# Feature-major latent queries, five whole gate blocks between the latent units, and T sums in quarters, in a hybrid decoder layer

## The chip, the cores and the metric

The kernel runs on one core of a Trainium2 chip. A core has TensorE (PE in the profile, with its weight loads as PEld), VectorE (DVE), ScalarE (ACT), GpSimd (POOL) and SyncE (SP), which here only issues DMAs; ACT issues some too. All DMAs run on the core's 16 DMA engines. The metric is the time of one execution in device microseconds (us), as the median of a few runs; lower is better.

## The reference, cut to what matters

One layer on 1024 tokens of width 1024, all in float32. Two token mixers run in parallel on `h = rmsnorm(x)`: sparse attention (NSA), and latent attention (MLA). Their outputs are merged by sigmoid gates, and a gated ConvFFN follows.

```python
proj = h @ w_in                       # 1024 x 3768: q_n, kv_n, gate_n, c_q, c_kv, k_r, merge
gm = sigmoid(merge)                   # 2048 columns: 16 blocks of 128, the "gate blocks"
q = (rmsnorm(c_q, g_q) @ w_uq).reshape(B, T, 8, 64 + 32)      # latent queries, 256 -> 768
q_rope = rope(q[..., 64:], cos, sin)  # x1*cos - x2*sin, x2*cos + x1*sin, halves of 16
kv = (rmsnorm(c_kv, g_kv) @ w_ukv).reshape(B, T, 8, 64 + 64)  # k_nope and v, 128 -> 1024
s = (q_nope @ k_nope.T + q_rope @ rope(k_r).T) * 96 ** -0.5   # causal softmax, then @ v
merged = gm[0] * (o_nsa @ w_br_nsa) + gm[1] * (o_mla @ w_br_mla)
```

## The kernel before, in words

Precision. Every large product is made of three fp32r matmuls (`mm3`, lines 303 to 305): an operand is split into a rounded high part (ACT copies it, L308) and a low part, the difference (DVE, L309; both in `split_evac`). For weights of class `Weights` the two instructions are L106 and L107.

Order. The kernel is written as a sequence of loops, but a planner sorts the instructions of each engine by priority (the written order) and by when it thinks that their inputs are ready. The run order is thus near the written one without being equal to it. Each engine then works in order. Tiles come from pools; a pool opened after others were closed takes their space, and its tiles wait for the old tiles that lay there. Left-side and right-side pools grow towards one another.

Stages up to the change. (1) The loop over the eight 128-token tiles: `prep(t)` normalises a tile and transposes it to feature-major `hh`/`hl` (high and low, two halves of 512 tokens), `tok1(t)` computes gate_n, c_q, c_kv and k_r, and `tok1_tr(t)` transposes the latents to `cth`/`ctl` (three chunks of 128 features by 1024 tokens). `xn` is a two-buffer tile of that loop. Positions give `sin` and `cos` with tokens on partitions. (2) `fproj(merge_evac(0))`: gate block 0. A whole gate block is two halves of 512 tokens, each of 8 x 3 matmuls of 512 columns; ACT takes the sigmoid, and the block goes to `gm_d` in DRAM by a DMA from ACT. (3) The latent stage, from `a2 = Pool("a2")`. For each token tile `mla_q` makes 8 x 96 query features with tokens on partitions (two matmul groups of 384 columns), ACT scales them into `qm` (L609), six DVE instructions turn the rotary part (L615 to L620), `mla_qt` transposes the eight heads (L627) and stores both parts to `q_d` in runs of 512 bytes (L630). `mla_v` makes the values of a token tile and stores them to `v_d`, by heads, in runs of 512 bytes (L639); `mla_k` makes the keys of two heads and 512 tokens and stores them to `k_d` in runs of 2 KB (L648). The store tiles `qx`, `vm`, `kx` have 3, 2 and 2 buffers. (4) Gate blocks. `EARLY` = 1, 2 and 13 are computed whole; blocks 3 to 12 in five pairs by class `Seven`, a seven-product scheme (Strassen-Winograd) over quarters: a product is 12 matmuls, a pair 84. It needs sums of the right operand, `t_block`: T1 = B12 - B11, T2 = B22 - T1, T3 = B22 - B12, T4 = B21 - T2, where B are quarters of `hh`/`hl`, and each T has four chunks of 512 columns. A chunk takes three DVE instructions (L675 to L677) and a split (L308, L309). For the weights, `block_sum` (L170) makes the S sums and `prep` the splits, in a ring of four. In the first pair the products come in the order P1, P2, P3, P5, P6, P7, P4 and need B11, B21, B22, T1, T2, T3, T4.

PSUM banks for single results come from `bank()`, three buffers (`pT`), and pairs of banks from `two_banks()`, two buffers (`sc`).

Weights. `Weights.get` splits an item and `ahead` more, and issues loads (L81, on SP's queue) for up to three raw buffers beyond, in the order in which the items were added. Split parts have two buffers.

Stages behind the change. Projections for NSA, its attention, then MLA attention in 15 visits of heads (`mla_unit`). `mla_load` (L1059 to L1062) fetches a head's keys, queries and values on SP's queue, one visit ahead; a tile is free for the visit after next. The output branches follow, then the ConvFFN and the rest, which the change doesn't touch.

Of the kernel before, what the change touches and what calls it, by code (L numbers as in the profile page):

```python
# [17 lines left out]
T = 1024  # L18
# [257 lines left out]
def tile_hybrid_layer(ctx: ExitStack, tc: tile.TileContext, x, p, positions, g_pre_mix, w_in,  # L276
# [81 lines left out]
    EARLY, PAIRED = (1, 2, 13), range(3, 13)  # L358
# [57 lines left out]
    gmp = Pool("gmp", side="right")  # L416
    a0 = Pool("a0", side="right")
# [130 lines left out]

    def fproj2(evacs):
# [35 lines left out]

    a2 = Pool("a2", side="right")
    wuh, wul = a2([128, 2, 768], F32R, "wuh"), a2([128, 2, 768], F32R, "wul")
    wkh, wkl, wvh, wvl = (a2([128, 8, 64], F32R, n) for n in ("wkh", "wkl", "wvh", "wvl"))
    scale_m = float(96.0 ** -0.5)

# [5 lines left out]
    for k, it in enumerate(uq_items):  # L596
        it.alloc = into(wuh[:, k], wul[:, k])
# [3 lines left out]
    def mla_q(t):  # L601
        ts = slice(t * 128, (t + 1) * 128)
        qm = a2([128, 8, 96], F32, "qm", bufs=3)
        for hf in range(2):
            ps = bank()
            hs = slice(hf * 384, (hf + 1) * 384)
            for k in range(2):
                mm3(ps[:, :384], cth[:, k, ts], ctl[:, k, ts], wuh[:, k, hs], wul[:, k, hs], k == 0, k == 1)
            nc.scalar.activation(qm[:, 4 * hf:4 * hf + 4], ps[:, :384].rearrange("p (h d) -> p h d", d=96),  # L609
                                 AF.Copy, scale=scale_m)  # L610
        x1, x2 = qm[:, :, 64:80], qm[:, :, 80:96]
        cb = cos[:, t, None, :].to_broadcast([128, 8, 16])
        sb = sin[:, t, None, :].to_broadcast([128, 8, 16])
        ra, rb = (a2([128, 8, 32], F32, n, bufs=2) for n in ("ra", "rb"))
        nc.vector.tensor_tensor(ra[:, :, :16], x1, cb, op=OP.mult)  # L615
        nc.vector.tensor_tensor(ra[:, :, 16:], x2, cb, op=OP.mult)
        nc.vector.tensor_tensor(rb[:, :, :16], x2, sb, op=OP.mult)
        nc.vector.tensor_tensor(rb[:, :, 16:], x1, sb, op=OP.mult)
        nc.vector.tensor_sub(x1, ra[:, :, :16], rb[:, :, :16])
        nc.vector.tensor_add(x2, ra[:, :, 16:], rb[:, :, 16:])  # L620
        return qm

    def mla_qt(t, qm):
        ts = slice(t * 128, (t + 1) * 128)
        ps = two_banks().rearrange("p a (b m) -> p (a b) m", m=128)
        for h in range(8):
            nc.tensor.transpose(ps[:96, h], qm[:, h], ident)  # L627
        qx = a2([96, 8, 2, 128], F32R, "qx", bufs=3)
        split_evac(qx[:, :, 0], qx[:, :, 1], ps[:96])
        nc.sync.dma_start(q_d.rearrange("h n p t -> p (h n) t")[:, :, ts], f32(qx).rearrange("p h n t -> p (h n) t"))  # L630

    def mla_v(t):
        ts = slice(t * 128, (t + 1) * 128)
        ps = bank()
        vh, vl = (w.rearrange("p h d -> p (h d)") for w in (wvh, wvl))
        mm3(ps, cth[:, 2, ts], ctl[:, 2, ts], vh, vl, True, True)
        vm = a2([128, 8, 128], F32R, "vm", bufs=2)
        split_evac(vm[:, :, 0:64], vm[:, :, 64:128], ps.rearrange("p (h d) -> p h d", d=64))
        nc.sync.dma_start(v_d.rearrange("h t p d -> t p h d")[t], f32(vm))  # L639

    def mla_k(pr, c):
        cs = slice(c * 512, (c + 1) * 512)
        ps = bank()
        wh, wl = (w[:, 2 * pr:2 * pr + 2].rearrange("p h d -> p (h d)") for w in (wkh, wkl))
        mm3(ps, wh, wl, cth[:, 2, cs], ctl[:, 2, cs], True, True)
        kx = a2([128, 2, 512], F32R, "kx", bufs=2)
        split_evac(kx[:, 0], kx[:, 1], ps)
        nc.sync.dma_start(k_d[pr].rearrange("n p t -> p n t")[:, :, cs], f32(kx))  # L648

    qms = {t: mla_q(t) for t in range(2)}  # L650
    for t in range(NT):
        mla_v(t)
        if t + 2 < NT:
            qms[t + 2] = mla_q(t + 2)
        mla_k(t % 4, t // 4)
        mla_qt(t, qms.pop(t))
# [4 lines left out]
    eA = Pool("eA", side="left")  # L661
    ringA = Pool("ringA", side="left")
    tA = Pool("tA", side="left")
    BA = {n: [tA([128, 4, 512], F32R, n + tag) for tag in "hl"] for n in ("T2", "T3", "T4", "T1")}
# [6 lines left out]
    def t_block(out_, plus, minus):  # L671
        for k in range(4):
# [5 lines left out]
            split_evac(BA[out_][0][:, k], BA[out_][1][:, k], sum_)  # L678

    fproj(merge_evac(EARLY[0]))  # L680
    t_block("T1", "B12", "B11")
    fproj(merge_evac(EARLY[1]))
    t_block("T2", "B22", "T1")
    fproj(merge_evac(EARLY[2]))
# [1093 lines left out]
```

## Time and profile before

| What | Value |
|---|---|
| Median of 3 runs | 1789.68 us (1784.37 to 1800.34) |
| The profiled execution | 1789.02 us; span in the trace 1787.2 us; mean granted clock 0.986 |
| Busy, share of the span | PE 96%, PEld 79%, DVE 71%, ACT 48%, POOL 16% |
| DMA | 191.94 MB, mean 107 GB/s |
| Chain that ended last, by engine | PE 80%, DVE 8%, DMA 7%, ACT 2% |

The span is the time from the first to the last instruction in the trace; the execution's own time holds 1.8 us around it. A line number such as L309 is a line of the kernel before, and a helper's line stands for all its callers, so groups are told apart by their tiles. PE counts as busy while a matmul is in the array, and neighbouring matmuls overlap, so the time from one start to the next is the better price of a matmul.

### The profile page before, as it was taken

What the parts mean: (1) busy time and instruction counts of PE and PEld (TensorE: products, weight loads), DVE (VectorE), ACT (ScalarE), POOL (GpSimd) and SP (SyncE); (2) the same over time, 40 slices, a digit from 0 to 9 for tenths busy, and PEclk for the clock granted to TensorE, in tenths of its full rate; (3) what the DMA queues carried; (4) which work ended last, traced back from release to release, by engine and by line L of the source; (5) the groups of instructions that cost most, each with busy time, mean ns of one, the idle gap of its engine ahead of it and who ended that gap; (6) DMA issues with size and microseconds to landing.
All of it is one profiled execution on the core that took longest, in us unless ns stands there. A gap on an engine that the chain in (4) does not pass through costs nothing.

```text
span 1787.2 us, 23559 instructions
## 1 busy us (share of the span) xinstructions
PE 1713.3 (96%) x8537; PEld 1403.3 (79%) x8537; DVE 1272.1 (71%) x2030; ACT 860.8 (48%) x1537; POOL 292.1 (16%) x435
## 2 busy tenths in 40 slices
PE   8969899999999999999899999999999998999998
PEld 7857688887777787887678887888888876887886
DVE  6557754425888887787765698888888879767553
ACT  6433332325777766666543354444444443345321
POOL 3000004003555544333401000000000000001010
PEclk8989899999999999999999999999999999999999
DMA  5295242200001225656383112222223292438111
GB/s 194 80 243 154 71 134 69 59 25 30 1 1 37 89 70 158 149 151 183 110 261 109 57 55 83 83 83 94 71 83 94 71 348 87 147 122 274 58 59 47
DMA packets 182512, 191.94 MB, mean 107 GB/s; under 512 B 12805, under 2 KB 136125, under 8 KB 182397
## 3 DMA queue, kind: packets, MB, share of 16 engines
q1 hardware_dynamic: 175292, 180.91, 33.2%
q10 hardware_dynamic: 7104, 9.54, 1.5%
q8 instruction: 67, 1.10, 0.2%
q14 instruction: 49, 0.39, 0.1%
HBM read 142.96 MB, written 47.45 MB: 107 GB/s over the span
## 4 chain that ended last, share of the span: by engine, by line
PE 80%; DVE 8%; DMA 7%; ACT 2%; issue 2%; SPq 1%; POOL 1%; DVEq 0%; POOLq 0%; ACTq 0%
PE big L304 9%; PE big L303 9%; PE big L305 9%; PE pT L303 6%; PE pT L304 6%; PE pT L305 6%; PE pT L885 5%; PE one L303 3%; PE one L304 3%; PE one L305 3%; PE oT L895 3%; PE oT L894 3%; DMA k_d<-kx 1%; DVE wlo L309 1%; PE sc L948 1%
## 5 line engine op out<-in xcount | busy, mean ns | idle before, releaser
L345 POOL TENSOR_SCALAR stat<-stat 128x1 f32<-128x1 f32 (+1 forms) x48 | 18.2, 380 | 892.5 <-ACT yn L1278 624.9
L309 DVE TENSOR_TENSOR pl<-pT,ph 128x512 fp32r<-128x512 f32 (+1 forms) x244 | 149.6, 630 | 13.7 <-ACT ph L308 12.2
L308 ACT ACTIVATE ph<-pT 128x512 fp32r<-128x512 f32 (+1 forms) x244 | 130.1, 555 | 60.7 <-PE pT L885 52.9
L303 PE MATMUL big<-hh,rh 128*128 128x512 f32 x380 | 148.2, 390 | 2.5 <-ACT e L220 1.0
L304 PE MATMUL big<-hl,rh 128*128 128x512 f32 x380 | 148.0, 389 | 0.0
L305 PE MATMUL big<-hh,rl 128*128 128x512 f32 x380 | 147.5, 389 | 0.0
L869 DVE TENSOR_REDUCE mx<-sc 128x1 f32<-128x640 f32 (+7 forms) x128 | 106.6, 835 | 32.4 <-PE sc L948 22.6
L308 ACT ACTIVATE rh<-S 128x512 fp32r<-128x512 f32 x100 | 62.8, 629 | 115.3 <-PE big L304 78.0
L1401 DVE SCALAR_TENSOR_TENSOR u<-C,wcT,u 128x1024 f32<-128x1024 f32 x88 | 111.0, 1280 | 3.7 <-ACT u L1397 3.2
L308 ACT ACTIVATE rh<-wraw 128x512 fp32r<-128x512 f32 x83 | 51.9, 630 | 114.2 <-PE big L304 47.1
L304 PE MATMUL big<-wlo,whi 128*128 128x512 f32 x242 | 97.0, 401 | 9.9 <-DVE wlo L309 9.9
L305 PE MATMUL big<-whi,wlo 128*128 128x512 f32 x242 | 95.2, 393 | 0.0
L303 PE MATMUL pT<-hh,whi 128*128 128x512 f32 x224 | 89.8, 401 | 5.1 <-DVE kx L309 3.3
L303 PE MATMUL big<-whi 128*128 128x512 f32 x242 | 91.3, 393 | 2.4 <-ACT whi L308 2.4
L304 PE MATMUL pT<-hl,whi 128*128 128x512 f32 x224 | 89.0, 397 | 0.0
L305 PE MATMUL pT<-hh,wlo 128*128 128x512 f32 x224 | 88.9, 398 | 0.0
L303 PEld LDWEIGHTS big<-hh,rh 128*128 128x128 f32 x380 | 71.2, 188 | 18.6 <-ACT e L220 1.5
L309 DVE TENSOR_TENSOR rl<-S,rh 128x512 fp32r<-128x512 f32 x100 | 68.7, 689 | 22.0 <-ACT rh L308 21.9
L304 PEld LDWEIGHTS big<-hl,rh 128*128 128x128 f32 x380 | 71.4, 188 | 15.0 <-DVE hl L309 0.4
L305 PEld LDWEIGHTS big<-hh,rl 128*128 128x128 f32 x380 | 71.4, 188 | 14.8
L308 ACT ACTIVATE whi<-wraw 128x1024 fp32r<-128x1024 f32 x40 | 42.1, 1058 | 53.0 <-DVE wraw L1463 20.9
L304 PEld LDWEIGHTS big<-wlo,whi 128*128 128x128 f32 x242 | 45.9, 190 | 24.7 <-DVE wlo L309 15.4
(543 smaller groups left out, 5003.2 us busy)
## 6 DMA issues: line engine op xcount, KB each, us to landing
wraw<-in_w_up_dram SPq DMA_DIRECT2D x44, 512.0 KB, 3.9
wraw<-in_w_in_dram SPq DMA_DIRECT2D x24, 512.0 KB, 4.7
g<-gm_d SPq DMA_DIRECT2D x48, 256.0 KB, 3.4
wraw<-in_w_down_dram SPq DMA_DIRECT2D x47, 256.0 KB, 3.3
g_d<-u SPq DMA_DIRECT2D x22, 512.0 KB, 2.6
wraw<-g_d SPq DMA_DIRECT2D x36, 256.0 KB, 3.0
xt<-in_x_dram SPq DMA_DIRECT2D x16, 512.0 KB, 6.8
gm_d<-gms ACTq DMA_DIRECT2D x16, 512.0 KB, 2.9
```

Of the source, the lines that this page charges most:

```text
L303: nc.tensor.matmul(ps, lh, rh, start=start, stop=False, skip_group_check=more)
L304: nc.tensor.matmul(ps, lh, rl, start=False, stop=False, skip_group_check=more)
L305: nc.tensor.matmul(ps, ll, rh, start=False, stop=stop, skip_group_check=more)
L308: nc.scalar.activation(hi, ps, AF.Copy)
L309: nc.vector.tensor_sub(lo, ps, f32(hi))
L345: nc.gpsimd.tensor_scalar(st, st, EPS, None, op0=OP.add)
L869: nc.vector.tensor_reduce(u.nm[:, r:r + 1], src, axis=AX.XY, op=OP.max, negate=True)
L885: nc.tensor.transpose(pT[:m, r], cols(r), ident)
L894: nc.tensor.matmul(oT[:, a:], v, ph, start=first, stop=False)
L895: nc.tensor.matmul(oT[:, a:], v, pl, start=False, stop=last)
L948: nc.tensor.matmul(ps[:, si, :w], q_part(0, 128, i, 4 * g + r), KA[b - 1][g][:, k0 + o:k0 + o + w], start=False, stop=True)
L1401: nc.vector.scalar_tensor_tensor(u[s], C[s][:, 2 - sh:2 - sh + T], wcT[:, 2 - sh, ch:ch + 1], u[s], op0=OP.mult, op1=OP.add)
```

## The change

The gate blocks computed whole are five, 1, 2, 13, 3 and 4; four pairs are left (blocks 5 to 12). Each whole block is cut into two halves (`fsteps`), and the ten halves are called between the units of the latent stage and between quarters of the T sums.

The latent queries are computed feature-major: the weights `w_uq`, scaled, are regrouped into `wn` (64 features a head, two heads to a block of 128) and `wr` (for four heads, 64 first-half rotary features, then 64 second-half ones). `q_nope` and `q_rope` give 128 features by 512 tokens, with no transposes. For the rotary part new tables `ctab` and `stab` hold cos and signed sin with features on partitions; `tables()`, called in the token loop at t = 5, makes them by 16 transposes. Queries are stored to `qn_d` and `qr_d` in runs of 2 KB. Values are stored to `v_d` token by token, 4 KB a token. All stores of the stage share a tile `st` with six buffers. `mla_load` fetches the queries with three DMAs: 64 partitions of `qn_d`, and twice 16 of `qr_d`.

The T sums are made a chunk of 512 columns at a time: `t_first(k)` makes T1 and T2, `t_second(k)` T3 = T2 - B11 and T4 = B21 - T2 from the unrounded T2, kept in `t2` (four buffers), so that T1 and T2 together take five DVE instructions and two splits, T3 and T4 four and two. `t_first` is called once in each of the four k/v turns, `t_second` behind them. The output tiles of `Seven.pair` take the `t2` buffers, four in place of five.

```diff
-    EARLY, PAIRED = (1, 2, 13), range(3, 13)
+    EARLY, PAIRED = (1, 2, 13, 3, 4), range(5, 13)
...
-    q_d = dram([8, 2, 96, T], F32, "q_d")
+    qn_d = dram([4, 2, 128, T], F32, "qn_d")
+    qr_d = dram([2, 2, 128, T], F32, "qr_d")
...
-    v_d = dram([8, NT, 128, 128], F32, "v_d")
+    v_d = dram([NT, 128, 8 * 128], F32, "v_d")
...
+    def tables():
+
+        for dst, src, sign in ((ctab, cos, 1.0), (stab, sin, -1.0)):
+            rep = a1([128, D], F32, "xn", bufs=2).rearrange("p (t r f) -> p t r f", r=8, f=16)
+            b = src[:, :, None, :].to_broadcast([128, NT, 4, 16])
+            nc.scalar.activation(rep[:, :, :4], b, AF.Copy)
+            nc.scalar.activation(rep[:, :, 4:], b, AF.Copy, scale=sign)
+            ps = two_banks().rearrange("p a (b m) -> p (a b) m", m=128)
+            for t in range(NT):
+                nc.tensor.transpose(ps[:, t], rep[:, t].rearrange("p r f -> p (r f)"), ident)
+            nc.vector.tensor_copy(dst.rearrange("p (t m) -> p t m", m=128), ps)
+
+    def fsteps(evac):
...
+        def half(c):
+            def run():
+                if c == 0:
+                    hold.extend(a.rearrange("p (k m) -> p k m", m=128) for a in W.get())
+                ps = bank()
+                for k in range(NK):
+                    mm3(ps, hold[0][:, k], hold[1][:, k], hh[c][:, k], hl[c][:, k], k == 0, k == NK - 1)
+                evac(c, slice(c * 512, (c + 1) * 512), ps)
+            return run
+        return [half(0), half(1)]
...
+        if t == 5:
+            tables()
...
+    def uq_split(k):
+        def scaled(hi, lo, src):
+            nc.scalar.activation(hi, src, AF.Copy, scale=scale_m)
+            nc.vector.scalar_tensor_tensor(lo, src, scale_m, f32(hi), op0=OP.mult, op1=OP.subtract)
...
+            scaled(*(w[:, k].rearrange("p (h d) -> p h d", d=64) for w in wn), r[:, :, :64])
+            for g in range(2):
+                for s in range(2):
+                    scaled(*(w[:, k, g, s] for w in wr), r[:, 4 * g:4 * g + 4, 64 + 16 * s:80 + 16 * s])
...
+    def parts_out(src, dst):
+        st_ = a2([128, 2, 512], F32R, "st", bufs=6)
+        split_evac(st_[:, 0], st_[:, 1], src)
+        nc.sync.dma_start(dst, f32(st_))
+
+    def q_block(wh, wl, c):
+        ps = bank()
+        for k in range(2):
+            mm3(ps, wh[:, k], wl[:, k], cth[:, k, half(c)], ctl[:, k, half(c)], k == 0, k == 1)
+        return ps
...
+    def q_rope(g, c):
+        def run():
+            ps = q_block(*(w[:, :, g].rearrange("p k s h f -> p k (s h f)") for w in wr), c)
+            ta, tx = (aq([128, 512], F32, n, bufs=2) for n in ("ta", "tx"))
+            nc.vector.tensor_mul(ta, ps, ctab[:, half(c)])
+            nc.vector.tensor_mul(tx[64:128], ps[0:64], stab[0:64, half(c)])
+            nc.vector.tensor_mul(tx[0:64], ps[64:128], stab[64:128, half(c)])
+            nc.vector.tensor_add(ta, ta, tx)
+            parts_out(ta, qr_d[g].rearrange("n p t -> p n t")[:, :, half(c)])
+        return run
...
+            nc.sync.dma_start(v_d[t], f32(vm).rearrange("p h d -> p (h d)"))
...
+    def t_first(k):
+
+        def run():
+            (b11, b12, b22) = ([f32(b[:, k]) for b in BA[n]] for n in ("B11", "B12", "B22"))
+            e = eA([128, 512], F32, "e")
+            t2 = t2s[k] = eA([128, 512], F32, "t2", bufs=4)
+            nc.vector.tensor_tensor(e, b12[0], b11[0], op=OP.subtract)
+            nc.vector.tensor_tensor(e, e, b12[1], op=OP.add)
+            nc.vector.tensor_tensor(e, e, b11[1], op=OP.subtract)
+            nc.vector.tensor_tensor(t2, b22[0], e, op=OP.subtract)
+            nc.vector.tensor_tensor(t2, t2, b22[1], op=OP.add)
+            split_evac(BA["T1"][0][:, k], BA["T1"][1][:, k], e)
+            split_evac(BA["T2"][0][:, k], BA["T2"][1][:, k], t2)
+        return run
...
+    early = [f for m in EARLY for f in fsteps(merge_evac(m))]
+    for i in range(4):
+        c, g = i // 2, i % 2
+        for f in (q_nope(2 * g, c), q_rope(g, c), q_nope(2 * g + 1, c)):
+            f()
+        early.pop(0)()
+    aq.close()
+    tb.close()
+    eA = Pool("eA", side="left")
+    tA = Pool("tA", side="left")
...
+    for i in range(4):
+        for f in (mla_k(i, 0), mla_v(2 * i), mla_k(i, 1), mla_v(2 * i + 1)):
+            f()
+        t_first(i)()
+        early.pop(0)()
+    a2.close()
+    a0.close()
...
+    for k in range(4):
+        t_second(k)()
+        if k % 2:
+            early.pop(0)()
     for i in range(4):
         gates7.block_sum(0, i)
     for n in range(Seven.RING):
         gates7.prep(n)
-    t_block("T3", "B22", "B12")
-    t_block("T4", "B21", "T2")
...
-        nc.sync.dma_start(f32(tl[0:96, 0:2, qs]), q_d[h].rearrange("n p t -> p n t")[:, :, qs])
-        nc.sync.dma_start(f32(vm[:, :n // 128]), v_d[h, :n // 128].rearrange("t p d -> p t d"))
+        nc.sync.dma_start(f32(tl[0:64, 0:2, qs]),
+                          qn_d[h // 2, :, h % 2 * 64:h % 2 * 64 + 64].rearrange("n p t -> p n t")[:, :, qs])
+        for s in range(2):
+            r0 = 64 * s + h % 4 * 16
+            nc.sync.dma_start(f32(tl[64 + 16 * s:80 + 16 * s, 0:2, qs]),
+                              qr_d[h // 4, :, r0:r0 + 16].rearrange("n p t -> p n t")[:, :, qs])
+        nc.sync.dma_start(f32(vm[:, :n // 128]),
+                          v_d[:n // 128, :, h * 128:h * 128 + 128].rearrange("t p d -> p t d"))
```

## Rows read from the trace of the kernel before

**Rows 1.** The page, part 2: granted TensorE clock, 40 slices, in tenths.

```profile
PEclk8989899999999999999999999999999999999999
```

**Rows 2.** Stretches: length; busy PE, PEld, DVE, ACT, POOL; clock; DMA share; GB/s.

```profile
80.00:85.00 5.00, 5.00 (x30) 4.86 (x29) 2.57 (x6) 4.01 (x7) 0.00 (x0) 1.00 1.02 281
...
130.00:135.00 5.00, 1.72 (x4) 0.90 (x4) 1.74 (x2) 0.60 (x1) 0.00 (x0) 0.50 0.94 241
...
174.00:197.00 23.00, 15.68 (x51) 10.94 (x51) 22.89 (x38) 8.60 (x15) 0.00 (x0) 0.78 0.09 23
```

**Rows 3.** Waits from 79 to 134.6 us: total us, times, longest us.

```profile
ACT kx L308 <- DMA k_d<-kx: 10.9, 4, 4.1
...
ACT vm L308 <- DMA v_d<-vm: 10.1, 3, 5.6
```

**Rows 4.** Groups, 79 to 134.6 us: busy us, mean ns, idle before.

```profile
L303 PE MATMUL pT<-wuh,cth 128*128 128x384 f32 x32 | 11.4, 363 | 2.7 <-ACT qm L609 1.8 <-DVE kx L309 1.0
...
L627 PE MATMUL sc<-ident,qm 128*96 128x128 f32 x64 | 9.2, 292 | 1.1 <-DVE qm L620 1.1
```

**Rows 5.** Timeline of PE, 79 to 144 us: start, us, instruction.

```profile
79.00 0.51 PE L303 MATMUL pT<-wuh,cth 128*128 128x384 f32 x2
...
81.11 0.33 PE L303 MATMUL pT<-wuh,cth 128*128 128x384 f32 x1
...
81.28 0.33 PE L304 MATMUL pT<-wul,cth 128*128 128x384 f32 x1
...
134.59 0.80 PE L303 MATMUL pT<-hh,whi 128*128 128x512 f32 x1 [3.28 <-DVE kx L309]
...
138.60 0.44 PE L303 MATMUL pT<-hh,whi 128*128 128x512 f32 x1
...
143.00 0.39 PE L304 MATMUL pT<-hl,whi 128*128 128x512 f32 x1
...
143.23 0.39 PE L305 MATMUL pT<-hh,wlo 128*128 128x512 f32 x1
```

**Rows 6.** Chain that ended last, in order of time: start us, us, what.

```profile
86.84 0.87 PE sc L627 x8
```

**Rows 7.** DMA, 76 to 170 us: packets, MB, share; one issue.

```profile
q1 hardware_dynamic: 31232, 18.88, 74.5%
q10 hardware_dynamic: 432, 1.57, 4.2%
...
k_d<-kx SPq DMA_DIRECT2D x8, 512.0 KB, 10.4
```

**Rows 8.** Timeline of PE around the T sums, 172 to 196 us.

```profile
174.73 0.39 PE L303 MATMUL pT<-T2h,rh 128*128 128x512 f32 x1
...
184.84 0.79 PE L304 MATMUL pT<-T3l,rh 128*128 128x512 f32 x1 [4.25 <-DVE T3l L309]
...
188.45 0.80 PE L304 MATMUL pT<-T3l,rh 128*128 128x512 f32 x1 [1.55 <-DVE T3l L309]
...
195.83 0.39 PE L305 MATMUL sc<-hh,rl 128*128 128x512 f32 x1
```

**Rows 9.** Timeline of DVE at 146 us, two neighbours.

```profile
145.62 0.69 DVE L170 TENSOR_TENSOR S<-wraw 128x512 f32<-128x512 f32 x1
146.22 0.69 DVE L309 TENSOR_TENSOR rl<-wraw,rh 128x512 fp32r<-128x512 f32 x1
```

**Rows 10.** Head load on SP, use on PE; landing of q_d, k_d loads.

```profile
718.41 0.59 SPq L1061 DMA_DIRECT2D hl<-q_d  x1
...
729.45 0.40 PE L1090 MATMUL sc<-hl 96*128 96x320 f32 x1
...
DMA to landing us min/median/max: 5.9/7.1/7.2
...
DMA to landing us min/median/max: 3.7/5.1/6.7
```

**Rows 11.** Timeline of PE in the last pair of gate blocks.

```profile
268.13 0.39 PE L303 MATMUL pT<-hh,whi 128*128 128x512 f32 x1
```

More of the change, by code (lines that the diff above doesn't have):

```diff
@@ L596, in tile_hybrid_layer @@
     for k, it in enumerate(uq_items):
-        it.alloc = into(wuh[:, k], wul[:, k])
+        it.alloc = uq_split(k)
     ukv_item.alloc = ukv_split
     take(uq_items + [ukv_item])
[L601 to L604, printed above, removed]
-            ps = bank()
[L606 to L639, printed above, removed]
@@ L641, in mla_k @@
-    def mla_k(pr, c):
[L642 to L656, printed above, removed]
@@ L657, in tile_hybrid_layer, with half @@
-    a2.close()
-    a0.close()
[L661 to L664, printed above, removed]
+    def half(c):
+        return slice(c * 512, (c + 1) * 512)
+    def parts_out(src, dst):
[7 more added lines that the diff above has]
+        return ps
@@ new lines, in q_nope @@
+    def q_nope(b, c):
+        def run():
+            ps = q_block(*(w[:, :, b * 128:(b + 1) * 128] for w in wn), c)
+            parts_out(ps, qn_d[b].rearrange("n p t -> p n t")[:, :, half(c)])
+        return run
[8 more added lines that the diff above has]
+            parts_out(ta, qr_d[g].rearrange("n p t -> p n t")[:, :, half(c)])
+        return run
@@ new lines, in mla_k, with run @@
+    def mla_k(pr, c):
+        def run():
+            ps = bank()
+            wh, wl = (w[:, 2 * pr:2 * pr + 2].rearrange("p h d -> p (h d)") for w in (wkh, wkl))
+            mm3(ps, wh, wl, cth[:, 2, half(c)], ctl[:, 2, half(c)], True, True)
+            parts_out(ps, k_d[pr].rearrange("n p t -> p n t")[:, :, half(c)])
+        return run
+    def t_first(k):
+        def run():
+            (b11, b12, b22) = ([f32(b[:, k]) for b in BA[n]] for n in ("B11", "B12", "B22"))
[8 more added lines that the diff above has]
+            split_evac(BA["T2"][0][:, k], BA["T2"][1][:, k], t2)
+        return run
@@ new lines, in t_second, with run @@
+    def t_second(k):
+        def run():
+            (b11, b21) = ([f32(b[:, k]) for b in BA[n]] for n in ("B11", "B21"))
+            e, t2 = eA([128, 512], F32, "e"), t2s[k]
+            nc.vector.tensor_tensor(e, t2, b11[0], op=OP.subtract)
+            nc.vector.tensor_tensor(e, e, b11[1], op=OP.subtract)
+            nc.vector.tensor_tensor(t2, b21[0], t2, op=OP.subtract)
+            nc.vector.tensor_tensor(t2, t2, b21[1], op=OP.add)
+            split_evac(BA["T3"][0][:, k], BA["T3"][1][:, k], e)
+            split_evac(BA["T4"][0][:, k], BA["T4"][1][:, k], t2)
+        return run
@@ L665, in tile_hybrid_layer @@
+    BA, t2s = {}, {}
     for c in range(2):
@@ L698, in tile_hybrid_layer @@
         nc.scalar.dma_start(gm_d[PAIRED[2 * f]], tl[0])
-    for pl in (tA, ringA, eA):
+    for pl in (tB, ringA, tA, eA):
         pl.close()
```

38 lines of the change are left out of this document (23 added, 15 removed).

## The prediction

> **What bounds the kernel now.** I read the page first, for its rows in 40 slices (44.7 us each): PE is the bound almost everywhere, and the granted clock is full except early on. Slices 3 and 5, where it dips [rows 1], hold the code that the change touches, so I then took the table of stretches. The reader is to see three things in it [rows 2]: from 80 to 85 us the DMA engines are already full while PE is busy; from 130 to 135 us PE works 1.72 us of 5 at half clock while the DMA share stays at 0.94; and from 174 to 197 us PE works 15.68 us of 23 while DVE works 22.89. So there are two holes with different owners. The table of waits names the first [rows 3]: ACT waits 10.9 us for k_d stores and 10.1 us for v_d stores to leave their tiles; PE then waits for a PSUM bank through DVE. Stores of the latent stage bind it. The second hole belongs to the T sums on DVE: PE waits for T3l [rows 8].
>
> What the holes cost on PE. At full clock a 512-column matmul starts every 0.227 us (143.00 to 143.23) and a 384-column one every 0.173 us; a fp32 transpose takes 0.87/8 = 0.109 us [rows 5, 6]. The latent stage runs from 79.00 to 134.59, 55.6 us [rows 5]. Its work is 96 matmuls of 384 columns (three lines of 32, [rows 4]) = 16.6 us, 48 of 512 for v and k = 10.9 us, and 64 transposes = 7.0 us: 34.5 us. Lost: 21.1 us. [...] Lost: 2.0 us. From P6 of the first pair to P1 of it, 174.73 to 195.83, 41 matmuls take 21.1 us in place of 9.3 [rows 8]. Lost: 11.8 us. Together 34.9 us, the most that better cover alone can return.
>
> **The change, part by part.**
> Query units. Twelve units (eight q_nope, four q_rope) of six 512-column matmuls replace the 16 token-major groups of six: 72 x 0.227 = 16.3 us against 16.6. No change. The 64 transposes go: PE gains 7.0 us. The rotary part becomes four units of three products from PSUM, one add and one difference, each 512 wide: DVE starts one such instruction every 0.60 us (145.62 to 146.22) [rows 9], so 3.0 us a unit. That lies under PE's whole gate half.
>
> Tables. 16 transposes on PE, 1.7 us, in the token loop, which PE bounds; ACT makes their four inputs just before, so I add 0.6 us for that wait: 2.3 us. Ends: 0 if the planner drops them into an idle moment, 4 us if PE waits for all four ACT instructions. The split of the query weights becomes ten small instructions in place of two on ACT and on DVE; it lies under the 48 matmuls of gate block 0 and costs nothing there (3 us if that cover failed).
>
> One pair fewer. A pair is 7 x 12 = 84 matmuls, two whole blocks are 96: 12 x 0.227 = 2.7 us more on PE. This is certain.
>
> Whole blocks between the units. A query turn is now 18 unit matmuls and 24 of a gate half, 9.5 us; a k/v turn 12 and 24, 8.2 us; four of each. The stores are the same 14.7 MB, but in runs of 2 KB (q, k) and 4 KB (v) where q and v had 512 B. Between 76 and 170 us queue q1, mostly 512 B runs, took 74.5% of 16 x 94 us for 31232 packets: 36 ns each of 604 B, 269 GB/s; q10, runs near 4 KB, took 146 ns for 3.6 KB, 398 GB/s [rows 7]. A line through the two gives about 89 ns for 2 KB, an estimate: 1.4 us for a 512 KB store. A query turn then asks for three stores, half a weight load (1.0 us) and half a gate store (0.7 us): 5.9 of 9.5 us. A k/v turn asks for 7.1 of 8.2 us. The stores stop binding, so the 21.1 and 2.0 us go. At the lower bound, with runs no faster than now, a k/v turn needs 9.4 us: 5 us come back over four turns.
> [...]
>
> What is late next is DVE. In a k/v turn it has 4 differences, 7 instructions of T1 and T2 and half a weight split: 7.2 us of 0.60 us steps, against PE's 8.2; but the seven stand in one block in front of the next turn's evacuations, and the ring of three banks is short. Between 0 and 2.4 us over four turns; I take 1.5. The T sums themselves shrink from 64 DVE instructions (38.4 us) to 52 (31.2 us): 28 in the k/v turns, 24 (14.4 us) behind them with only two gate halves (10.9 us) beside them. Counted from the last rotary unit DVE has 9.6 (k, v) + 2.4 (splits) + 31.2 + 2.4 (S sums) + 0.6 (first weight split of P1) + 2.4 of waits for ACT (an estimate, 0.3 per sum) = 48.6 us; PE has 5.5 + 32.7 + 10.9 = 49.0 us. That is level. If DVE runs ahead where it can, PE waits for nothing; if T3 and T4 stand whole behind the last turn, the first P1 comes 14.4 + 3.0 + 1.2 - 10.9 = 7.7 us late, and by the order of the pools its ring tiles follow the store tiles in the same space, so they can hardly be filled earlier. I take 4 us and 1 us of lower clock after it. T3 is wanted five products (13.6 us) later still and is no longer waited for. The output ring shrinks from five to four tiles, which is what the first pair holds: nothing.
>
> Heads' loads. Each visit loads its queries with three DMAs in place of one, two issues of about 0.6 us more on SP. The last load is issued at 718.41, lands 7.1 us later (the median), 725.5, and is first used at 729.45 [rows 10]: 3.9 us to spare. Cost nothing; later by 1.2 us it still fits.
>
> Sum: 34.9 + 7.0 - 2.7 - 2.3 - 1.5 - 5.0 = 30.4 us. The profiled execution took 1789.0 us (span 1787.2 and 1.8 around it), 0.7 under the median shown of 1789.7. So 1758.6 by its own time and **1759** for a median.
>
> **Rivals.**
> DVE binds the new stage: the blocks of seven hold back evacuations (2.4) and P1 waits in full (7.7 and 2 of low clock), tables at 4: 34.9 + 7.0 - 2.7 - 4 - 12.1 = 23.1, **1767**. For it: DVE was already full from 174 to 197 us [rows 2], and the two counts above are level. Against it: 12 instructions fewer, and idle DVE time in the query turns.
>
> The stores bind still: 5 us in the k/v turns, and the ring tiles free some 5 us later: 30.4 - 10 = 20.4, **1769**. For it: six store tiles, and landing took 10.4 us [rows 7]. Against it: the rates of the two queues.
>
> The change doesn't do what it says: the run order is a planner's. At 268.13 a matmul of the block after the gates (pT<-hh,whi) already runs inside the last pair [rows 11]. If the gate halves gather in the query turns and leave the 16 k/v units bare, those take DVE's 9.6 + 16.8 + 1.2 = 27.6 us against 10.9 on PE: 16.7 us lost in place of the 1.5: 15.2 of the gain, **1774**.
>
> Slower: the heads' loads. If each rotary quarter lands after the one before it, with the shortest landing of a k_d load, 3.7 us [rows 10], the queries come 7.4 us later against 3.9 spare: PE waits 3.5 us in each of 14 visits, 49 us, **1808**. It decides from 3.9 us of delay and turns the sign from about 6.1 us (30.4/14 = 2.2 more). For it: 16-partition slices are new. Against it: the DMA share is moderate there and the loads are issued without waiting for one another. [...]
>
> **How the numbers follow.** Forecast 0.60 (own range 1750 to 1764: all new waits at nothing gives 1789.7 - 36.9 = 1753; the lower end has the tables in a gap too), DVE 0.18, stores 0.08, bare units 0.10, slower 0.04. The range reaches from 1750 to 1775, which leaves out the slower case and tails of the others. Three runs of the kernel spread over 0.9%, so about 1% is what can be told from no change: 1% faster is under 1771.8. All of the first two, the stores case and a little of the bare units lie there: faster 0.88; within 1% 0.08, slower 0.04.
>
> **What would show it.** Right: no transposes of qm; PEclk at 1.00 from 80 us to the pairs; stores of qn_d and v_d landing in under 6 us; no wait of ACT for stores; the last pair's matmuls done some 30 us earlier, and everything behind shifted by the same amount. A wait of PE before the first P1 of 3 to 5 us on DVE or ACT is expected; 8 or more means the DVE rival. Waits of ACT for k_d or v_d mean the stores rival. Wrong altogether: the span from 300 us on grows, with PE waiting for qr_d loads in the head visits.

## The result, and the profile after

The changed kernel takes 1766.0 us (median of 4 runs, 1762.2 to 1770.4) against 1789.7 for the kernel before: a ratio of 0.9867, 95% interval 0.9841 to 0.9892, so 1.3% faster. The forecast was 1759, with 1750 to 1775 as its range. The profiled execution of after took 1762.18 us (span 1760.5, mean granted clock 0.994), 26.7 us less span than before; the medians give 23.7.

A mark behind the gate blocks tells what the changed stages alone returned: the first evacuation of a kcT tile, which ACT does as soon as the last pair is done. First before, then after (the tile's own view; start times are the pair behind the colon):

```profile
L718 ACT ACTIVATE kcT<-pT x4: 576/589/599, 279.9 to 299.0; 128x512 f32<-128x512 f32 x4
```

```profile
L793 ACT ACTIVATE kcT<-pT x4: 579/589/600, 253.0 to 271.9; 128x512 f32<-128x512 f32 x4
```

It comes 26.9 us earlier; the forecast was 30.4. Nearly the whole shortfall of the profiled execution, 3.5 us, is thus in the changed stages, and the first work to be done is to find it there. The page's clock row of after, against [rows 1], has lost the dips of slices 3 and 5:

```profile
PEclk9999999999999999999999999999999999999999
```

The table of stretches of after (columns as in [rows 2]) shows the two holes closed: from 130 to 135 us PE is at full clock and works 4.23 us of 5, and from 174 to 197 it never stops, where it worked 15.68 us of 23. From 80 to 85 us little has changed: the DMA engines are nearly as full (0.96), and PE works all the time, in both kernels. New are the first row, with a clock of 0.86 just ahead of the stage, and the rows from 125 to 140, where PE works some 4 us of 5 while DVE works all 5; from 150 to 155 DVE does nothing at all.

```profile
66.00:78.00 12.00, 9.76 (x40) 7.49 (x39) 2.81 (x12) 3.16 (x12) 0.93 (x2) 0.86 0.02 4
80.00:85.00 5.00, 5.00 (x23) 4.13 (x22) 1.70 (x7) 2.70 (x5) 0.00 (x0) 1.00 0.96 235
...
125.00:130.00 5.00, 3.83 (x16) 2.86 (x17) 5.00 (x10) 1.85 (x4) 0.00 (x0) 1.00 0.90 262
130.00:135.00 5.00, 4.23 (x19) 3.18 (x17) 4.93 (x9) 1.79 (x4) 0.00 (x0) 1.00 0.83 333
135.00:140.00 5.00, 3.90 (x16) 2.94 (x17) 5.00 (x10) 2.55 (x5) 0.00 (x0) 1.00 0.44 167
150.00:155.00 5.00, 5.00 (x24) 4.14 (x23) 0.00 (x0) 1.11 (x2) 0.00 (x0) 1.00 0.94 374
174.00:197.00 23.00, 23.00 (x103) 19.06 (x102) 18.40 (x31) 10.04 (x18) 0.00 (x0) 1.00 0.20 69
```

The waits of after from 82 to 157 us (columns as in [rows 3]) hold no wait of ACT for a store any more. What PE waits for is an evacuation on DVE, and, once each, the turned query block (tx), a sigmoid (gms) and a weight low (wlo, 0.5 us):

```profile
PE pT L303 <- DVE st L309: 4.1, 4, 1.5
...
PE pT L303 <- DVE tx L675: 0.9, 1, 0.9
PE pT L303 <- ACT gms L600: 0.8, 1, 0.8
```

PE's timeline of after gives the stages: the first query unit, the first gate matmul behind it, the first k/v unit, its first late evacuation, the first gate matmul behind the last unit, the first P1.

```profile
82.06 0.39 PE L303 MATMUL pT<-cth,wnh 128*128 128x512 f32 x1
...
87.22 0.47 PE L303 MATMUL pT<-hh,whi 128*128 128x512 f32 x1 [0.92 <-DVE tx L675]
...
122.06 0.39 PE L303 MATMUL pT<-cth,wkh 128*128 128x512 f32 x1
...
125.93 0.50 PE L303 MATMUL pT<-wvh,cth 128*128 128x512 f32 x1 [1.28 <-DVE st L309]
...
156.67 0.40 PE L303 MATMUL pT<-hh,whi 128*128 128x512 f32 x1
...
173.04 0.39 PE L303 MATMUL sc<-hh,rh 128*128 128x512 f32 x1
```

At 0.227 us a matmul, the query turns (4 x 42 matmuls, 38.1 us) took 40.0: 1.9 lost. The k/v turns with three gate halves between them (120 matmuls, 27.2 us) took 34.6: 7.4 lost. From there to P1, 72 matmuls took 16.4 us and were due 16.3: nothing lost. With the stage's start 3.06 us later than before (79.00 in [rows 5]) that is 12.4 us of new losses against the 39.2 that holes, transposes and the missing pair were to bring: 26.8, which is what the mark shows. So the ledger closes (the waits of the profile name only 4.1 + 0.8 us of the 7.4, because they count from a modelled end, 0.39 us after a matmul's start, and leave out short ones), and the one entry far from its forecast is the 7.4, for which the forecast had 1.5.

DVE's timeline says what it did meanwhile. L705 to L709 are the sums of T1 and T2, L719 to L722 those of T3 and T4, L309 the lows; `st` is an evacuation on which a PSUM bank hangs.

```profile
123.46 0.69 DVE L705 TENSOR_TENSOR e<-hh,hh 128x512 f32<-128x512 f32 x1
124.06 1.22 DVE L107 TENSOR_TENSOR wlo<-wraw,whi 128x1024 fp32r<-128x1024 f32 x1
125.19 0.68 DVE L309 TENSOR_TENSOR st<-pT,st 128x512 fp32r<-128x512 f32 x1
125.79 0.68 DVE L706 TENSOR_TENSOR e<-e,hl 128x512 f32<-128x512 f32 x1
126.39 0.68 DVE L309 TENSOR_TENSOR st<-pT,st 128x512 fp32r<-128x512 f32 x1
...
135.72 0.69 DVE L705 TENSOR_TENSOR e<-hh,hh 128x512 f32<-128x512 f32 x1
136.32 1.28 DVE L309 TENSOR_TENSOR st<-pT,st 128x512 fp32r<-128x512 f32 x2
...
142.33 0.69 DVE L719 TENSOR_TENSOR e<-t,hh 128x512 f32<-128x512 f32 x1
...
155.12 2.05 DVE L309 TENSOR_TENSOR st<-pT,st 128x512 fp32r<-128x512 f32 x3 [5.45 <-ACT st L308]
```

The first sum of the fourth turn (135.72) runs ahead of the second turn's evacuations (136.32), and the first T3 sum, written behind the last turn, starts at 142.33. The inputs of these sums had been ready since the token loop, and the run order lets them go first. The units of the first three turns take 5.1, 5.2 and 4.8 us for 2.7 us of matmuls, and then DVE is idle for 5.45 us.

### The profile page after: what moved, and what is told of

It is laid out like the page before. It is cut to its first block, busy times and chain, and to the rows that moved or that the text cites. A ratio compares the mean times of both kernels' runs of the same rounds, so it can differ in the third digit from the quotient of the medians.

```text
span 1760.5 us, 23428 instructions
## 1 busy us (share of the span) xinstructions
PE 1700.8 (97%) x8477; PEld 1390.7 (79%) x8477; DVE 1261.3 (72%) x1986; ACT 853.0 (48%) x1532; POOL 300.9 (17%) x435
## 4 chain that ended last, share of the span: by engine, by line
PE 80%; DVE 9%; DMA 6%; ACT 3%; issue 2%; POOL 1%; SPq 1%; DVEq 0%; POOLq 0%; ACTq 0%
PE big L304 9%; PE big L303 9%; PE big L305 9%; PE pT L303 6%; PE pT L305 6%; PE pT L304 6%; PE pT L960 5%; PE one L303 3%; PE one L304 3%; PE one L305 3%; PE oT L970 3%; PE oT L969 3%; DVE wlo L309 1%; PE sc L1023 1%; PE sc L1016 1%
## 5 line engine op out<-in xcount | busy, mean ns | idle before, releaser
L309 DVE TENSOR_TENSOR pl<-pT,ph 128x512 fp32r<-128x512 f32 (+1 forms) x244 | 149.6, 629 | 13.6 <-ACT ph L308 12.0
L303 PE MATMUL pT<-hh,whi 128*128 128x512 f32 x256 | 100.9, 394 | 3.0 <-DVE Vc L309 1.5
L305 PE MATMUL pT<-hh,wlo 128*128 128x512 f32 x256 | 100.7, 393 | 0.5 <-DVE wlo L107 0.5
L304 PE MATMUL pT<-hl,whi 128*128 128x512 f32 x256 | 100.3, 392 | 0.0
L309 DVE TENSOR_TENSOR rl<-S,rh 128x512 fp32r<-128x512 f32 x96 | 65.6, 686 | 19.5 <-ACT rh L308 19.5
L304 PEld LDWEIGHTS big<-wlo,whi 128*128 128x128 f32 x242 | 45.4, 188 | 24.5 <-DVE wlo L309 15.5
```

The costliest lines, as they stand in the source:

```text
L303: nc.tensor.matmul(ps, lh, rh, start=start, stop=False, skip_group_check=more)
L304: nc.tensor.matmul(ps, lh, rl, start=False, stop=False, skip_group_check=more)
L305: nc.tensor.matmul(ps, ll, rh, start=False, stop=stop, skip_group_check=more)
L309: nc.vector.tensor_sub(lo, ps, f32(hi))
```

## The experiments

Except for the last three, each time is that of one profiled execution, so the stretches of the gate stage carry the verdict. The kernel before took 1791.45 us beside the held sums, the late tables, the short runs and the bare units, and 1789.88 beside the other four.

### Holding the T sums behind the evacuations

`t_first(i)` may go out on the engines only behind the last evacuation of its own turn.

```diff
-            split_evac(vm[:, :, 0:64], vm[:, :, 64:128], ...)
+            last[0] = split_evac(vm[:, :, 0:64], vm[:, :, 64:128], ...)
...
-        t_first(i)()
+        with tc.issue_after(last[0].ins):
+            t_first(i)()
```

> Only the order on DVE is changed: the T1 and T2 instructions of a k/v turn may not be issued before the last evacuation of that turn. In the changed kernel PE takes 122.06 to 148.15 us for three k/v turns' units and two gate halves, 26.1 us for 19.0 us of matmuls. Theory (DVE runs ahead): sums of later turns stand in front of evacuations, so here this stretch falls to 19 to 21 us, five to seven us come back there; and because T3 and T4 are then made later, PE waits 0 to 7 us ahead of the first P1, where it waited 0. Rival (stores or the three banks bind in a k/v turn, whatever DVE's order): the stretch stays at 25 to 27 us.

Measured: 1757.44 us, the mark at 249.8. Waits and timeline of PE in this run:

```profile
PE pT L303 <- DVE st L309: 2.4, 4, 1.0
```

```profile
121.95 0.39 PE L303 MATMUL pT<-cth,wkh 128*128 128x512 f32 x1
...
125.70 0.40 PE L303 MATMUL pT<-hh,whi 128*128 128x512 f32 x1
...
153.43 0.39 PE L303 MATMUL pT<-hh,whi 128*128 128x512 f32 x1
...
169.77 0.39 PE L303 MATMUL sc<-hh,rh 128*128 128x512 f32 x1
```

The turns take 31.5 us in place of 34.6, and P1 still waits for nothing. The first three turns with two halves went from 26.1 to 22.5 us. That is short of the forecast for them, so the order of the sums explains 3.2 us of the 7.4, not all. In this run seven T instructions stand in one block behind each turn, as the prediction had pictured it, and the stretch still loses 31.5 - 27.2 = 4.3 us. Not all of that is the block's. The first turn has no T instruction ahead of it (its units run from 121.95 to 125.70, the first sum starts at 127.14), and it loses 1.0 us all the same. What is left there is the burst of four units, with a weight low in front of their evacuations; how the rest divides between burst and block this run doesn't tell. DVE's timeline:

```profile
127.14 0.68 DVE L705 TENSOR_TENSOR e<-hh,hh 128x512 f32<-128x512 f32 x1
...
159.56 1.28 DVE L170 TENSOR_TENSOR S<-wraw 128x512 f32<-128x512 f32 x2
...
163.18 1.29 DVE L309 TENSOR_TENSOR rl<-wraw,rh 128x512 fp32r<-128x512 f32 x2
```

The last two rows bear on P1: its weight lows (rl) are done at 164.5, 5.3 us before it starts, in between instructions of T3 and T4.

### The T sums as they were

The four sums in whole blocks with three differences each, as in the kernel before, at the place of `t_second`; all the rest as changed.

```diff
-        t_first(i)()
...
-        t_second(k)()
+    t_block("T1", "B12", "B11")
+    early.pop(0)()
+    t_block("T2", "B22", "T1")
+    early.pop(0)()
...
+    t_block("T3", "B22", "B12")
+    t_block("T4", "B21", "T2")
```

> The changed kernel with the T sums of before: whole blocks T1, T2 behind the k/v turns, then S sums, then T3 and T4 from the rounded parts, 64 DVE instructions; the last two gate halves stand between T1, T2 and the S sums. Theory (quarters under the turns are what removed the wait inside the first pair): the k/v turns get 4 to 6 us shorter, and PE waits 8 to 15 us in the first pair for T1 to T4, with the lower clock after it; kcT 4 to 10 us later than 253.0. Rival (the two more halves and the planner's freedom hide the sums in any order): kcT at 250 to 254.

Measured: 1770.37 us, the mark at 258.9, 5.9 later than after. But the place was not the expected one: the first pair waits for nothing, and the turns take 42.6 us. PE's waits for DVE, and two rows of DVE's timeline, show why:

```profile
PE pT L303 <- DVE st L309: 8.3, 5, 3.4
```

```profile
131.44 2.49 DVE L761 TENSOR_TENSOR t<-hh,T1h 128x512 f32<-128x512 f32 x4
133.85 2.49 DVE L762 TENSOR_TENSOR t<-t,hl 128x512 f32<-128x512 f32 x4
```

Four chunks of T2 at a time run in the middle of the k/v units, though they are written behind them. The quarters are worth 8.0 us in the turns, 5.9 at the mark (in this run the stage had started 1.2 us earlier, and P1 to the mark took 0.9 us less). The waits for DVE are 4.2 us longer than after's; much of the rest goes with the lower clock that follows them, 0.66 from 125 to 130 us and from 140 to 145, where after has 1.00. It is the same mechanism as above, larger: where DVE has ready sums, it does them ahead of an evacuation that PE needs.

### The tables behind the token loop

`tables()` goes ahead of the last `tok1_tr`, and only behind the last matmul of `tok1`.

```diff
-        if t == 5:
-            tables()
+    with tc.issue_after(last_pe[0].ins):
+        tables()
     tok1_tr(NT - 1)
```

> The 16 transposes of the rotary tables are issued on PE behind the last token tile's matmuls, where PE waits 2.2 us for the last latents, and not in the loop. Theory: they fill that wait and keep PE active, so gate block 0 starts 1.4 us earlier and the stretch at the lower clock (70.3 to 73.6 us, 1.6 us) goes: the latent stage starts at 79.0 to 79.6 us in place of 82.06, and all behind it 2.4 to 3 us earlier. Rival: the tables cost their 1.7 us wherever they stand and the dip is chance: the stage starts at 81.5 to 82.5.

Measured: 1761.29 us; the latent stage starts at 79.76, 2.3 earlier than after, and the mark stands at 250.1. PE's wait for the last latents is in both kernels, after first (with the wait of before, 2.17 us at 67.29, it is the same wait), then this one, in which transposes of the tables (sc) run in it:

```profile
68.71 0.52 PE L545 MATMUL pT<-ident,cn 128*128 128x128 f32 x3 [2.18 <-DVE cn L528]
```

```profile
66.63 0.93 PE L563 MATMUL sc<-ident,xn 128*128 128x128 f32 x7
68.05 0.52 PE L547 MATMUL pT<-ident,cn 128*128 128x128 f32 x3 [0.49 <-DVE cn L530]
```

Seven of the 16 transposes run in the wait, the other nine just ahead of it, from 65.21 us. So the 2 us hole that was there all along takes much of this work, and the tables are nearly free: in the four executions with the tables there, the latent stage starts between 0.2 us ahead of the 79.00 of before and 0.9 behind it, in the eight with the tables in the loop 1.8 to 4.5 us behind. The granted clock behind the hole is 0.86 from 66 to 78 us in after (above), 1.00 here. Over all the runs of this study, that stretch had 0.86 in six of the eight executions with the tables in the loop, and 1.00 in the four with the tables in the hole. But it had 1.00 in the kernel before as well, with the same wait, so the wait alone doesn't decide it.

### Short runs for the values

`v_d` by heads again, that is 512-byte runs, all else as changed.

```diff
-    v_d = dram([NT, 128, 8 * 128], F32, "v_d")
+    v_d = dram([8, NT, 128, 128], F32, "v_d")
...
-            nc.sync.dma_start(v_d[t], f32(vm).rearrange("p h d -> p (h d)"))
+            nc.sync.dma_start(v_d.rearrange("h t p d -> t p h d")[t], f32(vm))
...
```

> Values go to DRAM in the order of before, by heads, in runs of 512 bytes in place of 4 KB; nothing else changes. Theory (stores no longer bind once gate halves stand between the units): landing of the v_d stores grows from 3 or 4 to 5 or more us, PE's k/v stretch and the total change by less than 1 us. Rival (run length is what freed the stage): the four k/v turns grow by 3 to 5 us.

Measured: 1763.15 us; the k/v turns 36.2 us in place of 34.6, the mark at 253.7. DMA queues and issues from 76 to 170 us, after first, then this run (packets, MB, share; and KB each, median us to landing):

```profile
q1 hardware_dynamic: 16817, 19.84, 62.9%
...
k_d<-st SPq DMA_DIRECT2D x8, 512.0 KB, 3.9
v_d<-st SPq DMA_DIRECT2D x8, 512.0 KB, 5.6
```

```profile
q1 hardware_dynamic: 23238, 19.45, 65.5%
...
v_d<-st SPq DMA_DIRECT2D x8, 512.0 KB, 5.9
```

Neither account had it. By packets, 0.655 and 0.629 of 16 x 94 us make 985 and 946 us of engine time: 42 ns for 837 bytes against 56 ns for 1180. Short runs do take more time, 2.4 us over all 16 engines (3.6 if the 0.39 MB that this window misses are added at after's rate), where the prediction's line through two queues (33 ns for 512 bytes, 163 for 4 KB) makes it 6.3. The sign is that of the two queues in [rows 7]; of the 6.3 us, 2.4 to 3.6 were measured. That any of it reaches PE isn't shown: no wait of this run's turns names a store, and PE waits for DVE less than in after (3.5 us, 4.1 there). The 1.6 us by which the turns grew go with a lower clock in the gate half behind the third turn: 0.70 from 145 to 150 us, where after has 1.00.

### No gate work between the units

All ten gate halves follow behind the last unit.

```diff
-        early.pop(0)()
...
-        t_first(i)()
-        early.pop(0)()
+        t_first(i)()
...
-        if k % 2:
-            early.pop(0)()
+    while early:
+        early.pop(0)()
```

> All ten gate halves stand behind the latent units and T sums in place of between them; same work. Theory (the halves are the cover): 28 units alone ask for 27 us of PE but 14.7 MB of stores, 38 us at 385 GB/s, and DVE for 50 us of evacuations and sums; the units take 45 to 60 us in place of 27, the lower clock comes back, and the kernel loses 15 to 30 us of the gain. Rival (run length and the missing transposes made the gain, cover is worth little): under 8 us lost.

Measured: 1775.81 us, the mark at 263.0, 10.0 later. The 72 + 48 matmuls of the units, 27.2 us, took 45.7: 24.9 for queries and 20.9 for keys and values. The stretch of the k/v units:

```profile
107.50:128.50 21.00, 14.64 (x50) 8.04 (x48) 20.57 (x35) 11.91 (x22) 0.00 (x0) 1.00 1.00 375
```

DVE is busy for 20.57 us of 21 and the DMA engines all the time, so bare units are bound by both at once, and this run can't rank them. ACT waits for stores again, 3.2 us for v_d and 1.1 for k_d, as it does nowhere in the stage of after. The units lost 18.5 us against 9.3 in after (1.9 + 7.4). Their 45.7 us are within the 45 to 60 of the theory; the 10.0 us lost at the mark lie between the two accounts. The lower clock came back in the query units (0.83 from 90 to 100 us), not in the k/v units.

The row gives one more thing: at a share of 1.00 the DMA engines move 375 GB/s here; at 1.02 they moved 281 in the kernel before [rows 2], and at 0.96 only 235 in after from 80 to 85 us. The size of the packets differs, 507 bytes in after's row and 2.3 KB here, but so does what they carry, so no run ties the rate to the size alone. First after from 80 to 85 us, then the bare units from 107.5 to 128.5:

```profile
DMA packets 2329, 1.18 MB, mean 235 GB/s; under 512 B 31, under 2 KB 2329, under 8 KB 2329
```

```profile
DMA packets 3418, 7.88 MB, mean 375 GB/s; under 512 B 229, under 2 KB 229, under 8 KB 3416
```

The short packets from 80 to 85 us are those of weight loads, in both kernels, not of the stage's stores: the first of these goes out at 89.08 us in after, and in the kernel before here:

```profile
87.44 0.37 SPq L639 DMA_DIRECT2D v_d<-vm  x1
```

### Five pairs, three whole blocks

Blocks 3 and 4 stay a pair; six gate halves are left, two for the query turns and four for the k/v turns.

```diff
-    EARLY, PAIRED = (1, 2, 13, 3, 4), range(5, 13)
+    EARLY, PAIRED = (1, 2, 13), range(3, 13)
...
-        early.pop(0)()
+        if i % 2:
+            early.pop(0)()
...
-        if k % 2:
-            early.pop(0)()
```

> The changed kernel with three whole blocks and five pairs as before: halves in query turns 2 and 4 and in all k/v turns, none beside T3 and T4. PE has 2.7 us less to do. Theory (cover is worth more than the pair): two query turns without a half lose 1 to 3 us, the first P1 and P7 wait 6 to 12 us for S sums and T3 on DVE; kcT 4 to 10 us later than 253.0. Rival (the pair's 2.7 us is all that counts): kcT at 250 to 251.

Measured: 1766.45 us, the mark at 260.0, 7.0 later than after although PE has 2.7 us less to do. The query turns took 35.0 us for 27.2 of work (7.8 lost, 1.9 in after), more than the 1 to 3 us expected, in part by a lower clock (0.73 from 90 to 95 us). Between the last k/v unit and P1 there is one gate half here, where after has three, and P1 waits, though for less than the 6 to 12 us expected; P7 waits for nothing. First ACT's timeline, then PE's:

```profile
155.00 0.60 ACT L600 ACTIVATE gms<-pT 128x512 f32<-128x512 f32 x1 [4.89 <-PE pT L305]
...
157.18 1.13 ACT L308 ACTIVATE rh<-wraw 128x512 fp32r<-128x512 f32 x2
```

```profile
157.85 0.79 PE L303 MATMUL sc<-hh,rh 128*128 128x512 f32 x1 [2.89 <-ACT rh L308]
```

P1 then runs at half clock (0.79 for a matmul of 0.39; the granted clock is 0.50 from 157.8 to 160 us). The wait is at the place that the prediction charged with 5 us, but it is of another make: P1's weight copy (rh) stands on ACT behind the sigmoid of the gate half just ahead of P1, and not behind whole sums T3 and T4. With two more gate halves in between, rh is done at 165.7 us in after, 7 us before P1.

### Both orders at once, and the work woven

The two edits of order together:

> The two edits e1 (sums behind the evacuations) and e2 (tables in the wait) together. Each acts on its own stretch: 3.2 and 2.9 us at the first evacuation of the block after the gates (kcT), 253.0 us in the changed kernel. If they add, it comes at 246.5 to 247.5 us; if the second only moves the first's waits (T sums then bind the first P1, which waited 0 in e1), at 248.5 to 250.

Measured: 1760.59 us, the mark at 246.2, 6.8 before after's: 3.2 and 2.9 add up, with 0.7 besides. But the time is only 1.6 us under that of after's profiled execution. The rest, 5.2 us, went behind the changed stages, where this execution has more of the lower clock: 0.97 from 300 to 400 us (below, after first) and 0.97 from 1600 to 1700, where after has 1.00, in stages that are the same in both.

```profile
300.00:400.00 100.00, 97.81 (x540) 84.04 (x539) 30.27 (x46) 30.92 (x52) 7.19 (x8) 1.00 0.13 39
```

```profile
300.00:400.00 100.00, 97.62 (x506) 82.22 (x506) 32.11 (x51) 33.06 (x57) 8.23 (x10) 0.97 0.11 35
```

Then, on top of both, each gate half of a k/v turn is cut into four pieces of six matmuls and `t_first` into four pieces, and one of each follows each unit (the loop that calls them; how the pieces are made is left out):

```diff
-        for f in (mla_k(i, 0), mla_v(2 * i), mla_k(i, 1), mla_v(2 * i + 1)):
+        gate = early.pop(0)[1](4)
+        for j, f in enumerate((mla_k(i, 0), mla_v(2 * i), mla_k(i, 1), mla_v(2 * i + 1))):
             f()
-        t_first(i)()
-        early.pop(0)()
+            gate[j]()
+            with tc.issue_after(last[0].ins):
+                t_first(i)(j)
```

> As e5, and in the k/v turns a gate half is cut into four quarters, one behind each unit, with a quarter of the T1 and T2 instructions behind each unit's evacuation. In e1 a k/v turn still loses about 1 us, since four units of 0.7 us of PE arrive in a row and each needs some 1.3 us of evacuation from three banks. Theory (the burst costs it): four turns' units and three halves take 27.2 to 28.5 us, where e1 took 31.5, and kcT comes 3 to 4 us before e5's. Rival (DVE's total binds): the turns shorten but PE waits as long at P1, P5 or P7, kcT within 1 us of e5's.

Measured: 1754.65 us, the mark at 245.0, 1.2 earlier than without the weave, between the two accounts and nearer the rival's. From the first k/v unit to P1 (192 matmuls, 43.6 us) after took 51.0 us, the held sums 47.8, both orders 47.9 and the weave 46.5: of the 7.4 us lost, 2.9 are left.

### Timed beside one another

After, the held sums and the weave on one chip, with seven runs of the kernel before (1788.91 us):

> The changed kernel once more, as the control for the two runs beside it. Theory: its profiled execution lies between 1762 and 1770 us, with the gate stage the same to within 0.5 us each time (first kcT evacuation at 253.0 us, k/v turns 34.6 us), so that what differs from execution to execution lies in the clock of the stages behind it. Rival: the gate stage itself varies by 2 us or more, and single looks at it prove little.

> The T sums held behind the last evacuation of their turn, timed. Theory: 3.2 us less in the k/v turns (34.6 to 31.5) is kept to the end: 3 us under the control of the same chip, ratio to before about 0.985. Rival: the 8.6 us that the single look showed were the clock of later stages, and with rounds no more than 1 us under the control is left.

> Tables behind the last token group, gate half and T sums woven between the k/v units, timed. Theory: its 8.0 us at the first kcT evacuation (253.0 to 245.0) are kept: 7 to 9 us under the control, 1757 to 1759 for a median, ratio to before about 0.982. Rival: the part of it that the low clock behind gave back in the look without the weave (2 to 4 us) is lost here as well: 4 to 6 us under the control.

| Kernel | Median us (4 runs) | Ratio to before, 95% | Mark | First k/v unit to P1 |
|---|---|---|---|---|
| after | 1764.37 (1761.66 to 1767.19) | 0.9857, 0.9812 to 0.9902 | 254.4 | 50.95 |
| sums held | 1759.26 (1758.14 to 1762.07) | 0.9832, 0.9795 to 0.9869 | 250.7 | 47.83 |
| woven, tables late | 1755.45 (1754.12 to 1758.21) | 0.9811, 0.9774 to 0.9848 | 246.5 | 46.47 |

The stretch from the first k/v unit to P1 repeats to 0.03 us between the two executions of each kernel, while the mark moves by 0.9 to 1.5 us, mostly because the latent stage starts 1.1 to 1.4 us later in the second execution of each. The second execution of after has a dip of the clock in the first of these gate halves (0.72 from 130 to 135 us) and loses nothing by it: the units behind it take 3.5 us in place of 5.2, since DVE has caught up meanwhile. The weave gains 8.9 us on after, and its slowest run is faster than after's fastest: it beats both kernels. The held sums gain 5.1, of which their stage shows 3.1 and 2.0 are not placed. Both profiled executions of after have a dip of PE's clock late in the head visits (the row of 832 to 836 us below, 0.57 in the other), and those of the held sums have none there, with visits 2 to 4 us shorter in all. But the dip doesn't follow the order of the sums: the run with the tables late alone, whose sums go as in after, has none (1.00 from 800 to 860 us) and visits shorter by 2.6 us, and the run with both orders, whose sums are held, has it (0.91 from 820 to 840 us, as in after). What brings it on stays open.

```profile
832.00:836.00 4.00, 4.00 (x15) 3.24 (x14) 3.45 (x9) 1.58 (x5) 1.78 (x2) 0.63 0.47 155
```

## Why the prediction came out as it did

**Holes, transposes, one pair fewer (34.9 + 7.0 - 2.7).** Right. No transposes of queries are left, PE runs without a gap from 156.67 us to well past P1 at full clock (1.00 from 157 to 173 us and from 174 to 197), and with the new losses counted the sum gives the mark to 0.1 us. The 2.0 us within the 34.9 belong to the matmuls behind the first hole: nine of them took the 4.0 us from 134.59 to 138.60 in before, at a granted clock of 0.50, where nine at 0.227 us make 2.0.

**Stores.** Right that they stop binding: k_d lands in 3.9 us where it took 10.4 [rows 7], and in the stage no wait names a store (behind it ACT waits for a v_d store once, 0.5 us). The full DMA engines of 80 to 85 us, which the prediction read beside the stores, were busy with weight loads. The rate behind the term was off: short runs cost less than the line through two queues said (2.4 to 3.6 us against 6.3), so part of the relief must lie elsewhere. The gate work between the stores is one part, since without it ACT waits for stores again (the bare units, 4.3 us); what the six shared store tiles add no run tells.

**Query units.** Priced as level, with no loss; 1.9 us were lost. The first gate half waits 0.92 us for the bank of the first turned block and 0.47 for a weight low. It is small, and the prediction had named no such wait.

**Tables (2.3).** Measured 3.06 in the profiled pair, of another make: some 1.4 us in the token loop and, behind an unchanged wait of 2.2 us, about 1.6 of lower clock, which two of eight executions didn't have. The run with the tables in that wait, 0.8 us behind before's start, shows that the term could have been near the prediction's lower end, 0.

**K/v turns (1.5).** This is the term that was mis-sized: 7.4 us. The step that failed is the sentence that the seven T instructions "stand in one block in front of the next turn's evacuations", with 2.4 us as its worst case. They don't stand in one block: the run order takes them as soon as their inputs are ready, one or two turns ahead, between the evacuations. The counts of DVE's work were right and level with PE's, but the sum was made over the whole stage, while the excess fell into its first 25 us and the slack (5.45 us idle) behind it. And the upper bound of 2.4 was too low as well: with the block as pictured (the run with the sums held) the turns still lose 4.3 us, 1.0 of them in a turn that has no block ahead of it. The burst of four units has a price of its own, for which the prediction had no term. Of the 7.4 us, holding the sums gave back 3.2 and the weave 1.4 more; the last 2.9 stay open. The rival with DVE as the bound had the engine right and kept 2.4 for this place; it looked for the rest at P1.

**P1 (5.0).** Nothing was lost. The prediction's own other branch came out, "If DVE runs ahead where it can, PE waits for nothing", but not only by what DVE had gained in the turns. With the sums held DVE makes T1 to T4 later, and P1 waits for nothing either: the S sums and P1's weight lows go in between the instructions of T3 and T4, and are done 5.3 us before P1 (5.8 in after). So T3 and T4 never "stand whole behind the last turn", and the 7.7 us from which the 5.0 was taken have no ground in these runs. That two errors nearly cancel is luck: together the two terms were 6.5 against 7.4 measured, which is why the total came near.

**Heads' loads (0).** Right. PE's longest waits from 640 to 880 us name ACT and DVE (1.0 us the longest), never a load. From 700 to 860 us the 64 KB rotary quarters land in 4.0 us (tile hh) and 6.3 (hl), medians, where the 256 KB of the same tiles, issued about 1 us before them, take 5.7 and 6.9. The last pair of slices goes out from 819.42 us and is first used at 836.63.

**The total.** At the mark, 26.9 of 30.4 came. The medians differ by 23.7 (first set) and 24.5 (last set): the prediction took the profiled execution for the median, and after's was the fastest of its four runs, 3.8 us under their median. So 1766 is above the forecast's own range (1750 to 1764), inside the whole one, and beside the 1767 of the DVE rival: the k/v turns, where PE's waits name DVE above all, hold 7.4 of the 12.4 us of new losses, while that rival put 7.7 + 2 us at P1, where nothing was lost, and 4 on the tables. That its number came out is luck too.

## What to carry to other kernels

Count an engine's work per turn and in the order in which it will run, not over the stage: a level sum hid 7.4 us lost on PE, with 5.45 us of idle DVE behind them. Work whose inputs are ready early can be taken early by a planner, as the T sums were here, and on the engine that evacuates PSUM it then goes in front of what the bound engine waits for; tie it behind the last evacuation of its turn (3.2 us here), and put it in small pieces between units (1.4 more). An old wait of PE is a place for new PE work: with the 16 transposes in the loop the latent stage started 1.8 to 4.5 us behind before's, with them in the wait and just ahead of it at most 0.9.

## What the runs showed of the hardware

After one and the same wait of 2.2 us PE's granted clock fell in some executions and not in others of the same kernel: the held sums had 0.86 from 66 to 78 us in one execution and 1.00 in the other. With the wait filled, seven transposes in it and nine ahead, it fell in none of four (1.00 from 66 to 78 us).

The DMA engines moved 235 GB/s at a share of 0.96 in packets of 507 bytes (after, 80 to 85 us, mostly weight loads) and 375 GB/s at a share of 1.00 in packets of 2.3 KB (the bare units from 107.5 to 128.5 us, mostly stores).

Dips of the clock in unchanged stages (300 to 400 us, 832 to 836) come to about 3 us and 1.5 us (0.97 over 100 us, 0.63 over 4), as much as the smaller edits here; a stretch between two marks repeated to 0.03 us from execution to execution and told those edits apart, one time of the whole kernel did not.
